# Gate and up projections as Strassen block products, and the down projection as its own stage

## The chip, the core and the metric

The kernel runs on one core of one Trainium2 chip. Its time is the device time of one execution in microseconds (us); three runs of the kernel before the change gave 3655.61 us as their median (3653.2 to 3656.53). The engines named here are TensorE (PE, matmuls; PEld is its loading of weights), VectorE (DVE), ScalarE (ACT), GpSimd (POOL) and SyncE (SP, which issues the loads; ACT issues the stores).

## The reference, cut to what matters

Two blocks run one after the other over 2048 tokens of width 1024. The change lies in the first block, from its output projection to its end:

```
mixed = concat(rmsnorm(ys), rmsnorm(yp))              # 512 + 512 features
h = h + mixed @ w_out                                 # 1024 x 1024
n2 = rmsnorm(h, norm2_g)
ff = silu(n2 @ w_gate) * (n2 @ w_up)                  # 1024 -> 2816 each
h = h + ff @ w_down                                   # 2816 -> 1024
out = rmsnorm(h, final_norm_g)                        # end of the first block
h2 = layer_norm(out, ln_in_g, ln_in_b)                # start of the second
proj = h2 @ w_in_2                                    # attention and linear attention follow
```

## The kernel before

All matrices lie with features on the 128 partitions and tokens along the free axis. A "block" is 512 tokens (`b` = 0 to 3), a "half" is two blocks (`i` = 0, 1), and a feature tile is 128 features (`KT` = 8 tiles of 1024, `NFF` = 22 tiles `j` of 2816). Every product is done to nearly full fp32 precision with three matmuls: each operand is split into a rounded high part and the rest, and `mm3` (L157) issues high by high, high by low, low by high for each k-tile, 128 x 128 weights against 512 tokens.

Weights come through `get_w` (L143) in the order of the generator `weights` (L112): a 512 KB load on SP into `wr` (two buffers), the high part on ACT (`wh`), the low part on POOL, or on DVE where the generator says so (`wl`). The list of instructions on each engine is put in order ahead of time by a scheduler which plays the program against its own timing of each engine; at run time every engine takes its list strictly in that order, and a wait in one instruction holds all behind it.

From 395 to 645 us runs the output projection of the mixer, `mix_out` (L855), one block at a time in the order 2, 3, 0, 1. `mix_in` (L815) loads the eight input tiles of the next block and splits them without the norm's factor; the two halves of the features go to two PSUM tiles, and each is multiplied by its own 1/rms row on the way out. Blocks 0 and 1 keep their result in the SBUF accumulators `hacc`, blocks 2 and 3 go to DRAM (`h1_d`).

From 645 to 2155 us runs the feed-forward part, `ffn_half` (L910) for half 0 and half 1. For each `j` and each block `i`, 24 matmuls make the gate (`pg`), 24 the up product (`pu`), both over eight k-tiles. DVE, ACT and POOL turn them into the hidden tile and split it (`hh`, `hl`). Every second `j`, `down` multiplies the last two hidden tiles by `w_down`: 32 PSUM tiles `dn` of six matmuls, half of them per block, each added on DVE to `hacc` by

```
self.stt(d, pt, 0.5, d, ALU.mult, ALU.add)
```

The hidden tiles never leave SBUF, and the 22 `w_down` tiles are loaded once per half. At the end of a half, `block_norm` (L971) does both norms in place on `hacc` and stores `h2_d`; its pieces are spread over the work that follows by `step`. `ffn_in` (L892) makes the split input of a half: 32 tiles.

From 2155 us on, `proj_half(0, 0)` (L1075) starts the second block.

## Time and profile before

| what | before |
|---|---|
| median of 3 runs | 3655.61 us |
| the profiled execution | 3662.77 us |
| its span, first to last instruction | 3660.8 us |
| PE busy | 3415.1 us (93%) |
| DVE busy | 2038.2 us (56%) |
| ACT busy | 1407.4 us (38%) |
| POOL busy | 1456.0 us (40%) |
| granted TensorE clock, mean | 0.972 |

Busy time of an engine is the union of its records. A matmul's record (some 390 ns for 512 columns) overlaps that of the next, since they are pipelined, so the pace of PE is read from a count over a stretch in which PE never waits, not from the length of a record. A DVE record includes the time in which the instruction was started but held up.

### The profile page before, as it was taken

How to read it: one execution, taken by the hardware profiler on the slowest of the kernel's cores; microseconds unless marked ns; L12 is line 12 of the kernel's file. 1: busy time of each engine (PE TensorE's matmuls, PEld its weight loads, DVE VectorE, ACT ScalarE, POOL GpSimd, SP SyncE). 2: the span in 40 equal slices, each digit the busy share in tenths (PEclk: the TensorE clock that was granted, in tenths of full speed). 3: DMA queues.
4: the chain of work that ended last, by engine and by line, in shares of the span. 5: the costliest groups of instructions: out<-in, count | busy, mean ns of one | idle time of the engine just before them, and what ended most of it. 6: DMA issues, size and time to landing. Idle time of an engine off the chain costs nothing.

```text
span 3660.8 us, 45396 instructions
## 1 busy us (share of the span) xinstructions
PE 3415.1 (93%) x16648; PEld 2838.1 (78%) x16648; DVE 2038.2 (56%) x3431; ACT 1407.4 (38%) x2494; POOL 1456.0 (40%) x1092
## 2 busy tenths in 40 slices
PE   6898798999999998899999989999999999989897
PEld 6687666888888886688888878798888987767676
DVE  7677799433333348533333366234665446787774
ACT  5344544211111125311111154234655445666653
POOL 1255455533343346334333343322322225353544
PEclk9999999999999999999999999999999999989898
DMA  8644554111111122311111135565665666555351
GB/s 246 135 125 117 153 180 130 59 51 48 41 58 46 41 94 91 132 41 58 47 47 51 41 104 190 159 175 171 175 174 148 170 174 174 162 145 157 111 170 51
DMA packets 275490, 424.90 MB, mean 116 GB/s; under 512 B 73506, under 2 KB 159026, under 8 KB 275268
## 3 DMA queue, kind: packets, MB, share of 16 engines
q1 hardware_dynamic: 194880, 334.79, 31.4%
q10 hardware_dynamic: 80388, 87.22, 7.4%
q8 instruction: 131, 2.15, 0.3%
q14 instruction: 91, 0.75, 0.1%
HBM read 324.63 MB, written 87.20 MB: 112 GB/s over the span
## 4 chain that ended last, share of the span: by engine, by line
PE 63%; DVE 15%; DMA 10%; issue 5%; ACT 5%; POOL 1%; SPq 1%; ACTq 0%; DVEq 0%; POOLq 0%
PE pg L161 5%; PE pg L162 5%; PE pg L163 5%; PE pt L163 4%; PE pt L161 4%; PE pt L162 4%; PE pu L161 4%; PE pu L163 4%; PE pu L162 4%; PE dn L161 4%; PE dn L162 4%; PE dn L163 4%; PE pv L1257 2%; PE s L1215 1%; PE pv L1091 1%
## 5 line engine op out<-in xcount | busy, mean ns | idle before, releaser
L44 POOL TENSOR_TENSOR wl<-wr,wh 128x1024 fp32r<-128x1024 f32 (+1 forms) x223 | 548.5, 2466 | 635.9 <-ACT wh L54 590.9
L54 ACT ACTIVATE wh<-wr 128x1024 fp32r<-128x1024 f32 (+2 forms) x297 | 308.0, 1045 | 684.6 <-PE dn L162 197.3
L51 DVE SCALAR_TENSOR_TENSOR hacc<-dn,hacc 128x512 f32<-128x512 f32 x352 | 242.4, 691 | 381.2 <-PE dn L163 379.8
L161 PE MATMUL pg<-xh,wh 128*128 128x512 f32 (+1 forms) x1000 | 390.9, 391 | 15.3 <-ACT t L54 13.6
L162 PE MATMUL pg<-xl,wh 128*128 128x512 f32 (+1 forms) x1000 | 389.2, 389 | 11.3 <-DVE xl L44 6.5
L163 PE MATMUL pg<-xh,wl 128*128 128x512 f32 (+1 forms) x1000 | 388.6, 389 | 1.5 <-POOL wl L44 1.5
L161 PE MATMUL pt<-xh,wh 128*128 128x512 f32 x896 | 358.8, 401 | 7.3 <-DVE t L51 4.3
L163 PE MATMUL pt<-xh,wl 128*128 128x512 f32 x896 | 357.4, 400 | 1.9 <-POOL wl L44 1.4
L162 PE MATMUL pt<-xl,wh 128*128 128x512 f32 x896 | 357.1, 399 | 0.0
L161 PE MATMUL dn<-hh,wh 128*128 128x512 f32 x704 | 278.9, 396 | 20.6 <-DVE hacc L51 13.5
L161 PE MATMUL pu<-xh,wh 128*128 128x512 f32 x704 | 278.6, 396 | 0.0
L162 PE MATMUL pu<-xl,wh 128*128 128x512 f32 x704 | 278.5, 396 | 0.0
L163 PE MATMUL dn<-hh,wl 128*128 128x512 f32 x704 | 275.3, 392 | 3.1 <-POOL wl L44 3.1
L163 PE MATMUL pu<-xh,wl 128*128 128x512 f32 x704 | 278.1, 395 | 0.0
L162 PE MATMUL dn<-hl,wh 128*128 128x512 f32 x704 | 276.1, 392 | 0.0
L48 POOL TENSOR_SCALAR P<-P,rsm 128x640 f32<-128x640 f32 (+4 forms) x128 | 103.3, 807 | 349.7 <-DVE rsm L1225 286.6
L161 PEld LDWEIGHTS pg<-xh,wh 128*128 128x128 f32 x1000 | 190.8, 191 | 59.0 <-ACT t L54 17.2
L162 PEld LDWEIGHTS pg<-xl,wh 128*128 128x128 f32 x1000 | 190.8, 191 | 50.2 <-DVE xl L44 6.9
L163 PEld LDWEIGHTS pg<-xh,wl 128*128 128x128 f32 x1000 | 190.5, 191 | 40.5 <-POOL wl L44 1.9
L44 POOL TENSOR_TENSOR raw<-raw,rb 128x512 f32<-128x512 f32 x88 | 115.2, 1309 | 252.9 <-DVE raw L51 252.9
L44 POOL TENSOR_TENSOR hl<-raw,hh 128x512 fp32r<-128x512 f32 x88 | 114.1, 1297 | 252.8 <-ACT hh L54 252.8
L44 DVE TENSOR_TENSOR t<-pg,rb 128x512 f32<-128x512 f32 x88 | 60.6, 689 | 267.0 <-PE pg L163 266.9
(427 smaller groups left out, 8067.3 us busy)
## 6 DMA issues: line engine op xcount, KB each, us to landing
wr<-in_w_out SPq DMA_DIRECT2D x64, 512.0 KB, 4.3
wr<-in_w_in SPq DMA_DIRECT2D x44, 512.0 KB, 4.0
wr<-in_w_gate SPq DMA_DIRECT2D x44, 512.0 KB, 3.5
wr<-in_w_up SPq DMA_DIRECT2D x44, 512.0 KB, 3.5
wr<-in_w_down SPq DMA_DIRECT2D x44, 512.0 KB, 3.5
raw<-h_d SPq DMA_DIRECT2D x80, 256.0 KB, 4.1
wr<-in_w_ple_gate SPq DMA_DIRECT2D x32, 512.0 KB, 4.0
K<-kh_d SPq DMA_DIRECT2D x48, 256.0 KB, 6.1
```

Source lines behind the costliest of these rows:

```text
L44: return (eng or self.dve).tensor_tensor(out=o, in0=x, in1=y, op=op)
L48: (eng or self.dve).tensor_scalar(out=o, in0=x, scalar1=s1, scalar2=s2, op0=op0, **kw)
L51: return self.dve.scalar_tensor_tensor(out=o, in0=x, scalar=s, in1=y, op0=op0, op1=op1)
L54: return self.act.activation(out=o, in_=x, func=func, **kw)
L161: self.pe.matmul(ps, lhsT=hi[k], rhs=xh[k], start=(first and k == 0), stop=False)
L162: self.pe.matmul(ps, lhsT=hi[k], rhs=xl[k], start=False, stop=False)
L163: self.pe.matmul(ps, lhsT=lo[k], rhs=xh[k], start=False, stop=(last and k == n - 1))
L1091: self.pe.matmul(pt, lhsT=xh, rhs=wlo[:, k % 4], start=False, stop=False)
L1215: self.pe.matmul(sp[:, j, 0:n], lhsT=QQ[:, q0:q0 + 128], rhs=kk[:, k0 + o:k0 + o + n], start=st, stop=not st)
L1257: self.pe.matmul(pv, lhsT=VH[:, kb + x - kt0], rhs=self.PT[m][ch][:, sl], start=(n == 0 and m == 0), stop=(n == len(idxs) - 1 and m == 1))
```

## The change

Gate and up together are one product of a 2 x 2 block matrix (rows: gate, up; columns: the lower and upper 512 input features) with a 2 x 2 block matrix (rows: the same halves of the features; columns: the two token blocks of a half). Strassen's scheme, in Winograd's form, gets the four results from seven block products instead of eight, with additions on the operands before and on the results after. `gu_in` makes the seven token-side operands of a half (56 split tiles instead of 32, each normed ahead of the split), `gu_w` the seven weight-side operands of a tile `j`, one tile ahead, and `gu_half` runs the products: 12 matmuls each, named `pa`, `pb`, `pc` by PSUM bank. `pa` holds the running sum of products 1, 6, 7, 4, and is read between them.

The hidden tiles go to DRAM (`hh_d`, `hl_d`, four stores of 256 KB per `j`). `down` runs after all 22 `j` of a half, one block at a time: it loads the hidden tiles of one `j` back and multiplies them by all eight tiles of `w_down`, which add up in eight PSUM banks over all 22 `j`; only then does DVE add the residual, which comes from DRAM. `w_down` is loaded once per block, four times in all. The result goes to DRAM (`h3_d`), and the final norm (`norm`) reads it from there three times per block, in small steps (`bg_step`) that are placed between the products of the next stage. `gu_in` of half 1 is placed in `down(0)` in the same way, `norm(0)` and `norm(1)` in `gu_half(1)`, `norm(2)` and `norm(3)` in `proj_half(0, 0)`. `mix_out` takes blocks 0 and 1 together, then 2, then 3; the norm's factor is applied to its input tiles, so that one PSUM tile collects all eight k-tiles.

```
+        for j in range(NFF):                       # gu_half
+            w = self.gw
+            nw = self.gu_w(j + 1) if j + 1 < NFF else iter(())
+            pa, pb = bank("pa"), bank("pb")
+            product(pa, 1, True, False)
+            s1 = self.tmp("t", 2)
+            self.fn(s1, pa, AF.Copy)
+            product(pb, 2, True, True)
+            self.tt(s1, pb, s1, ALU.add)
+            h0 = gated(s1)
+            next(nw, None)
+            product(pa, 6, False, False)
+            s2 = self.tmp("t", 2)
+            self.fn(s2, pa, AF.Copy)
+            pc = bank("pc")
+            product(pc, 5, True, False)
+            p5 = self.tmp("raw", 4)
+            self.fn(p5, pc, AF.Copy)
+            next(nw, None)
+            product(pa, 7, False, False)
+            self.tt(p5, pa, p5, ALU.add)
+            product(pc, 3, False, True)
+            self.tt(s2, pc, s2, ALU.add)
+            h1 = gated(s2)
+            next(nw, None)
+            self.tt(h1, h1, p5, ALU.mult)
+            put(1, h1)
+            self.bg_step()
+            product(pa, 4, False, True)
+            self.tt(h0, pa, h0, ALU.mult)
+            put(0, h0)
...
+        put(1, 2, *self.split_in(rg, self.wp, [128, KT, 128], 2, "", None))      # gu_w
+        self.tt(ru[:, lo4], rg[:, lo4], ru[:, lo4], ALU.subtract, eng=self.pool)
...
+        self.tt(s2, ru[:, hi4], ru[:, lo4], ALU.subtract)
...
+        self.halves((th, tl), s2)
+        self.tt(rg[:, lo4], rg[:, lo4], s2, ALU.add)
+        self.tt(rg[:, hi4], rg[:, hi4], s2, ALU.subtract)
...
+        self.halves((sh, sl), rg)
+        put(7, 4, *self.split_in(ru, self.wp, [128, KT, 128], 2, "", None))
...
+            b11, b12, b21, b22 = four                                            # gu_in, for k in range(4)
+            t1 = self.tmp("t", 2)
+            self.tt(t1, b12, b11, ALU.subtract)
+            self.halves(x[1], b11)
+            self.halves(x[2], b21)
+            self.tt(b11, b22, t1, ALU.subtract)
+            self.halves(x[6], b11, self.pool)
+            self.halves(x[5], t1)
+            self.tt(b12, b22, b12, ALU.subtract)
+            self.halves(x[7], b12)
+            self.halves(x[3], b22, self.pool)
+            self.tt(b21, b21, b11, ALU.subtract)
+            self.halves(x[4], b21)
...
+            for j in range(NFF):                                                 # down, for each block
+                hh = self.fp.tile([128, 512], F32R, tag="hh", name="hh", bufs=3)
+                hl = self.fp.tile([128, 512], F32R, tag="hl", name="hl", bufs=3)
+                self.load(hh.bitcast(F32), self.hh_d[b, j])
+                self.load(hl.bitcast(F32), self.hl_d[b, j])
+                hi, lo = self.get_w()
+                for m in range(KT):
...
+                    self.mm3(pss[m], [hi[:, m]], [lo[:, m]], [hh], [hl], first=j == 0, last=j == NFF - 1)
+                if i or j > 1:
+                    self.bg_step()
...
+            for m in range(KT):
+                h = self.tmp("raw", 4)
+                self.load(h, self.h1_d[m * 128:(m + 1) * 128, c])
+                self.stt(h, pss[m], 0.5, h, ALU.mult, ALU.add)
+                self.store(self.h3_d[m * 128:(m + 1) * 128, c], h)
```

What stands on DVE's list in the feed-forward part, before: from one reading of a gate tile to the next but one, with `t<-pg,rb` the reading of a gate, `raw<-raw,t` the gating, `raw<-raw,pu` the product with the up tile, `hacc<-dn,hacc` the adding of a down tile.

```order
L44 TENSOR_TENSOR t<-pg,rb 128x512
L51 SCALAR_TENSOR_TENSOR raw<-raw,t 128x512
L44 TENSOR_TENSOR raw<-raw,pu 128x512
L51 SCALAR_TENSOR_TENSOR hacc<-dn,hacc 128x512 x9
L44 TENSOR_TENSOR t<-pg,rb 128x512
L51 SCALAR_TENSOR_TENSOR raw<-raw,t 128x512
```

Now, in the middle of `gu_half(0)`, one whole tile `j`: `wtl`, `wr`, `sq`, `wsl` are the weight-side operands (`gu_w`).

```order
L44 TENSOR_TENSOR t<-pb,t 128x512
L51 SCALAR_TENSOR_TENSOR raw<-raw,t 128x512
L44 TENSOR_TENSOR wtl<-sq,wth 128x512
L44 TENSOR_TENSOR wr<-wr,sq 128x512 x2
L44 TENSOR_TENSOR sq<-wru 128x512
L44 TENSOR_TENSOR raw<-pa,raw 128x512
L44 TENSOR_TENSOR t<-pc,t 128x512
L44 TENSOR_TENSOR wsl<-wr,wsh 128x1024
L51 SCALAR_TENSOR_TENSOR raw<-raw,t 128x512
L44 TENSOR_TENSOR raw<-raw 128x512
L44 TENSOR_TENSOR raw<-pa,raw 128x512
```

The adding to `hacc` is gone from these lists; four instructions of a tile read PSUM (`pa`, `pb`, `pc`), and eight work from SBUF to SBUF. The same list early in `gu_half(1)`, from the reading of `pb` to the end of the weight-side operands of one tile, with `nh`, `mt`, `sl` of the final norm between them:

```order
L44 TENSOR_TENSOR t<-pb,t 128x512
L51 SCALAR_TENSOR_TENSOR raw<-raw,t 128x512
L44 TENSOR_TENSOR wtl<-sq,wth 128x512
L48 TENSOR_SCALAR mt<-st 128x512
L44 TENSOR_TENSOR wr<-wr,sq 128x512 x2
L44 TENSOR_TENSOR sl<-s,sq 128x512
L51 SCALAR_TENSOR_TENSOR nh<-nh,v_final_norm_g,mt 128x512 x2
L44 TENSOR_TENSOR raw<-pa,raw 128x512
L44 TENSOR_TENSOR t<-pc,t 128x512
L44 TENSOR_TENSOR sq<-wru 128x512
L51 SCALAR_TENSOR_TENSOR nh<-nh,v_final_norm_g,mt 128x512
L44 TENSOR_TENSOR wsl<-wr,wsh 128x1024
```

The norm's instructions stand ahead of those that read PSUM, and are taken first. POOL's list in the feed-forward part before, with `raw<-raw,rb` and `hl` of the hidden tile and `wl` of the weights:

```order
L44 TENSOR_TENSOR raw<-raw,rb 128x512
L44 TENSOR_TENSOR wl<-wr,wh 128x1024
L44 TENSOR_TENSOR hl<-raw,hh 128x512
L44 TENSOR_TENSOR raw<-raw,rb 128x512
L44 TENSOR_TENSOR hl<-raw,hh 128x512
```

And now, across the end of `gu_half(0)` into `down(0)`, where `xl` are operands of half 1 (`gu_in`):

```order
L44 TENSOR_TENSOR wl<-wr,wh 128x1024 x2
L44 TENSOR_TENSOR hl<-raw,hh 128x512 x2
L44 TENSOR_TENSOR wl<-wr,wh 128x1024
L44 TENSOR_TENSOR xl<-raw,xh 128x512 x2
L44 TENSOR_TENSOR wl<-wr,wh 128x1024 x2
```

Two operands of half 1 stand ahead of each of the next pairs of `w_down` tiles, four pairs in all. Last, SP's list as the mixer's output projection begins, before, with `yp_d` and `ys_d` the mixer's two results:

```order
L57 DMA wr<-in_w_out 128x1024 x2
L57 DMA raw<-yp_d 128x512 x4
L57 DMA wr<-in_w_out 128x1024 x2
L57 DMA raw<-ys_d 128x8x64 x4
L57 DMA raw<-in_x 128x512
```

and now:

```order
L57 DMA wr<-in_w_out 128x1024 x4
L57 DMA yr<-yp_d 128x512 x6
L57 DMA wru<-in_w_up 128x1024 x2
L57 DMA yr<-yp_d 128x512 x2
L57 DMA yr<-ys_d 128x8x64 x8
```

All four first tiles of `w_out` stand ahead of `yp_d` now; the third and fourth wait until the first two have been split, since `wr` has two buffers.

## Rows read from the trace of the kernel before

**Rows 1.** Busy time by stretch; columns: start:end, length, engines (x instructions), clock, DMA.

```profile
395.00:645.00 250.00, 206.21 (x811) 157.87 (x810) 223.40 (x235) 123.41 (x173) 136.56 (x84) 0.92 0.52 159
645.00:1340.00 695.00, 695.00 (x3018) 566.70 (x3017) 246.72 (x299) 122.89 (x155) 265.76 (x151) 1.00 0.15 49
1340.00:1430.00 90.00, 83.35 (x354) 65.20 (x352) 74.58 (x89) 47.88 (x72) 54.89 (x33) 1.00 0.39 123
1430.00:1530.00 100.00, 81.66 (x320) 62.79 (x321) 68.53 (x86) 45.44 (x60) 49.62 (x29) 0.91 0.39 133
1530.00:2100.00 570.00, 570.00 (x2476) 464.86 (x2475) 194.62 (x239) 94.29 (x120) 211.54 (x121) 1.00 0.15 49
2100.00:2155.00 55.00, 45.48 (x190) 34.77 (x189) 39.63 (x48) 30.77 (x51) 31.91 (x20) 0.99 0.37 115
2155.00:2310.00 155.00, 148.63 (x802) 128.83 (x803) 88.31 (x123) 57.30 (x108) 56.96 (x41) 0.96 0.45 152
1475.00:1500.00 25.00, 19.58 (x85) 15.56 (x83) 22.70 (x33) 16.74 (x22) 3.79 (x2) 0.97 0.68 232
```

**Rows 2.** The page's chain that ended last, shares by engine.

```profile
PE 63%; DVE 15%; DMA 10%; issue 5%; ACT 5%; POOL 1%; SPq 1%; ACTq 0%; DVEq 0%; POOLq 0%
```

**Rows 3.** Page, groups of instructions; count, busy us, mean ns, idle before and releaser.

```profile
L161 PE MATMUL dn<-hh,wh 128*128 128x512 f32 x704 | 278.9, 396 | 20.6 <-DVE hacc L51 13.5
L161 PE MATMUL pu<-xh,wh 128*128 128x512 f32 x704 | 278.6, 396 | 0.0
```

**Rows 4.** Groups of DVE, POOL, ACT, 645 to 1340 us, shapes apart; columns as rows 3.

```profile
L51 DVE SCALAR_TENSOR_TENSOR hacc<-dn,hacc 128x512 f32<-128x512 f32 x158 | 109.3, 692 | 192.9 <-PE dn L163 192.9
L51 DVE SCALAR_TENSOR_TENSOR raw<-raw,t 128x512 f32<-128x512 f32 x43 | 65.3, 1519 | 31.9 <-ACT raw L54 31.9
...
L44 POOL TENSOR_TENSOR wl<-wr,wh 128x1024 fp32r<-128x1024 f32 x63 | 152.2, 2425 | 172.4 <-ACT wh L54 161.1 <-PE dn L163 11.3
L44 POOL TENSOR_TENSOR raw<-raw,rb 128x512 f32<-128x512 f32 x43 | 56.1, 1304 | 115.1 <-DVE raw L51 115.1
L44 POOL TENSOR_TENSOR hl<-raw,hh 128x512 fp32r<-128x512 f32 x42 | 54.1, 1288 | 132.6 <-ACT hh L54 132.6
...
L54 ACT ACTIVATE wh<-wr 128x1024 fp32r<-128x1024 f32 x63 | 65.8, 1058 | 264.2 <-PE dn L162 92.8 <-DMA wr<-in_w_up 56.0 <-PE pg L162 45.5
```

**Rows 5.** DVE in order of time: start us, us, instruction; one `j`, then the mixer.

```profile
1018.33 2.47 DVE L51 SCALAR_TENSOR_TENSOR raw<-raw,t 128x512 f32<-128x512 f32 x1 [0.76 <-ACT raw L54]
...
1031.44 0.69 DVE L51 SCALAR_TENSOR_TENSOR raw<-raw,t 128x512 f32<-128x512 f32 x1 [0.70 <-ACT raw L54]
...
554.20 1.21 DVE L44 TENSOR_TENSOR wl<-wr,wh 128x1024 fp32r<-128x1024 f32 x1
...
557.36 1.82 DVE L44 TENSOR_TENSOR hacc<-hacc,raw 128x512 f32<-128x512 f32 x1
```

**Rows 6.** POOL in order of time at the same places.

```profile
1017.85 2.40 POOL L44 TENSOR_TENSOR wl<-wr,wh 128x1024 fp32r<-128x1024 f32 x1 [1.14 <-ACT wh L54]
...
554.85 1.70 POOL L44 TENSOR_TENSOR s<-s,sq 128x512 f32<-128x512 f32 x1 [0.62 <-ACT sq L54]
...
557.33 1.30 POOL L44 TENSOR_TENSOR s<-s,sq 128x512 f32<-128x512 f32 x1 [0.78 <-ACT sq L54]
```

**Rows 7.** The loads as the mixer's output projection begins, SP in order of time.

```profile
394.79 0.87 SPq L57 DMA_DIRECT2D wr<-in_w_out  x2
395.71 1.88 SPq L57 DMA_DIRECT2D raw<-yp_d  x4
```

**Rows 8.** Page, DMA issues: count, KB each, median us from issue to landing.

```profile
wr<-in_w_down SPq DMA_DIRECT2D x44, 512.0 KB, 3.5
raw<-h_d SPq DMA_DIRECT2D x80, 256.0 KB, 4.1
```

**Rows 9.** What PE waited for, 1400 to 2160 us: total us, times, longest.

```profile
PE dn L161 <- DVE hacc L51: 11.7, 5, 6.7
PE dn L161 <- ACT wh L54: 6.8, 2, 6.6
PE pv L1090 <- DVE hacc L51: 4.6, 1, 4.6
```

More of the change, by code (lines that the diff above doesn't have):

```diff
@@ L966, in load_acc, with bg_step @@
[L966 to L979 removed]
+    def bg_step(self, n=1):
+        while n and self.bg:
+            if next(self.bg[0], None) is None:
+                self.bg.pop(0)
+            else:
+                n -= 1
@@ new lines, in gu_prime, with gu_half, product, bank @@
+    def gu_prime(self):
+        self.gu_raws = [self.gu_raw(0)]
+        for _ in self.gu_w(0):
+            pass
+    def gu_half(self, half):
+        def product(ps, p, first, last):
+            hi, lo = w[p]
+            x = self.xg[p]
+            ks = range(4)
+            for k in ks:
+                for n, (l_, r_) in enumerate(((hi, 0), (hi, 1), (lo, 0))):
+                    self.pe.matmul(ps, lhsT=l_[:, k], rhs=x[k][r_], start=(first and k == n == 0),
+                                   stop=(k == 3 and n == 2), skip_group_check=True)
+        def bank(name):
+            return self.ps.tile([128, 512], F32, tag="ps", name=name, bufs=8)
+        def gated(g):
+            th = self.tmp("raw", 4)
+            self.fn(th, g, AF.Tanh, scale=0.5)
+            self.stt(th, th, 1.0, g, ALU.add, ALU.mult)
+            return th
+        def put(i, h):
+            hh = self.fp.tile([128, 512], F32R, tag="hh", name="hh", bufs=3)
+            hl = self.fp.tile([128, 512], F32R, tag="hl", name="hl", bufs=3)
+            self.split(hh, hl, h)
+            self.store(self.hh_d[2 * half + i, j], hh.bitcast(F32))
+            self.store(self.hl_d[2 * half + i, j], hl.bitcast(F32))
+        for j in range(NFF):
[25 more added lines that the diff above has]
+            put(1, h1)
+            self.bg_step()
+            product(pa, 4, False, True)
+            self.tt(h0, pa, h0, ALU.mult)
+            put(0, h0)
+            next(nw, None)
+            self.bg_step()
+            if j == NFF - 1:
+                self.w_all = self.weights(f"down{half}")
+                self.w_next.append(self.get_w(0))
@@ L1094, in tokens @@
                     done(cb, t0 + t * 128, pt)
+                    if half == part == 0:
+                        self.bg_step()
         def put_v(cb, t, pt):
```

417 lines of the change are left out of this document (233 added, 184 removed).

## Prediction

> **What bounds the kernel now.** I read the table of stretches first [rows 1]. From 645 to 1340 us and from 1530 to 2100 us PE is busy all the time at full clock while DVE, ACT and POOL are all under 40%: the feed-forward part is bound by the number of matmuls. Around the turn of the halves and at the end PE lacks 6.7 + 18.3 + 9.5 = 34 us of 245. The mixer's output projection, 395 to 645 us, is another matter: PE lacks 44 of 250 us and its clock averages 0.92 of 2.4 GHz, while DVE is busy 223 us and POOL 137 us, together more than the stretch is long. The chain [rows 2] gives PE 63% and DVE 15%, which fits a kernel with one long matmul stage and DVE in the short ones.
>
> The pace of PE: 695.00 us / 3018 matmuls = 0.2303 us each [rows 1]; the 390 ns of a record [rows 3] overlap.
>
> DVE and POOL shut each other out. A gating instruction from SBUF to SBUF takes 0.69 us alone, and 2.47 us when POOL has begun a 2.40 us split 0.5 us before it [rows 5, 6]: it ends 0.55 us after POOL does. It holds the other way too: a sum on POOL takes 1.30 us alone and 1.70 us beside the 1.21 us split on DVE [rows 5, 6]. Instructions that read PSUM are not held: the 158 adds to `hacc` mean 692 ns with POOL at 38%, the gating 1519 ns [rows 4]. So for two-input work in SBUF the two engines have one budget. The mixer's stretch confirms it: the lists hold 124 narrow DVE instructions for it (512 columns, 0.69 us) and 32 wide ones (1024 columns, 1.21), and with 84 POOL sums (1.29) they add up to 233 us of 250.
>
> **The matmuls.** Per tile `j` of a half, 7 products x 12 = 84 matmuls replace 96; 12 x 44 tiles = 528 fewer, x 0.2303 = **-121.6 us**. The down matmuls stay 2112, the mixer's 768. A tile `j` now lasts 84 x 0.2303 = 19.35 us, one `j` of `down` 24 x 0.2303 = 5.53 us.
>
> **The old waits go.** 645 to 2155 us is 1510 us; 6336 matmuls x 0.2303 = 1459. The other **-51 us** (waits, slower clock, column sums at the turns; for what PE waited see rows 9) belong to `hacc`, whose tiles had to be ready before the next adds and norms. The 352 adds of 0.69 us on DVE go too, beside PE in any case, worth nothing by themselves. What takes the place of both is costed below.
>
> **The mixer's output projection: +15 us.** By the same budget: 113 narrow and 12 wide on DVE, 52 sums and 12 splits (2.43) on POOL = 78 + 15 + 67 + 29 = 189 us, plus `gu_in(0)` with 52 on DVE and 8 on POOL = 46, plus the first weights of `gu_w`, 12: 247 us against 233, 14 more. Added to it, the `yp_d` loads, which began at 395.7 us [rows 7], now stand behind two more weight loads that wait for a split: some 5 us; taken off, the last operands, which PE needs a few products later: 4 us. Bounds: -20 (the budget was not quite full before, and PE has 44 us of waits to lose) to +35.
>
> **`gu_half(0)`: +3 us of waits.** Per tile, POOL has two wide splits, one narrow subtraction and two splits of hidden tiles: 2 x 2.43 + 1.30 + 2 x 1.29 = 8.7 us [rows 4]; DVE has seven narrow and one wide from SBUF, 7 x 0.69 + 1.21 = 6.0. That is 14.8 us of budget in 19.35 us; the four PSUM readers, 2.8 us, run beside POOL. It fits, at 77%. The hand-offs are tight: `pa` must be copied or read before the next product adds to it, within one product of 2.76 us, behind whatever stands ahead on DVE. One wide POOL split in the way costs 2.4 us. PE's list has pieces of the next tile's products 1 and 2 put in between, which roughly doubles the slack. Bounds 0 to 40 us (2 us per tile).
>
> **`gu_half(1)`: +52 us of waits.** Here `norm(0)` and `norm(1)` are laid over 14 of 22 tiles. They bring 88 narrow DVE instructions from SBUF and 28 sums on POOL: 88 x 0.69 + 28 x 1.29 = 97 us. In the lists, ten of the 14 tiles carry nearly all, 8.6 on DVE and 2.8 on POOL each: 14.8 + 5.9 + 3.6 = 24.3 us of budget for 19.35 us of matmuls, so these tiles are bound by DVE and POOL: 10 x 5.0 = 50, and a little for the column sums in PE's list. Bounds: 0 (the lists let the norms fall behind) to 110 (DVE also waits for PSUM in order, 3 us more per tile, and more at the sums).
>
> One rule of the Trainium skill speaks against this stage. With rows first: where PE was busy 82% its mean clock was 0.92 and 0.91, a mixture of 1.2 and 2.4 GHz, and where it was busy 93% it was 1.00 [rows 1]. The Trainium skill ("TensorE: Matmul & The Clock Gate", section "A second HAM failure mode: psum-queue depth-cycling") says that a kernel which cycles through PSUM banks and idles briefly between groups of matmuls can have its clock swing between half and full. By it the ten loaded tiles, busy 19.35 / 24.3 = 80%, would run at 0.92, and the sum would be up to 17 us higher if PE and not DVE set their length; by the budget alone it costs nothing, since the clock only fills PE's waits.
>
> **`down`.** PE has no partner that must follow each tile any more. Loads are 2 x 256 KB of hidden tiles and 512 KB of weights per 5.53 us, 190 GB/s; the trace shows 232 GB/s at 68% of the DMA engines [rows 1], and loads land in 3.5 and 4.1 us [rows 8] with two tiles of lead, so I cost the way through DRAM at nothing; each microsecond short per `j` would cost 88. The weights' split, 1.06 + 2.43 us [rows 4] after a buffer comes free, fits in 5.53. But `gu_in(1)` stands in `down(0)`: per k-tile 13 narrow on DVE and two on POOL, with two weight splits between, 9.0 + 2.6 + 4.9 = 16.5 us against two `j` of 11.1, and POOL's list makes the `w_down` splits wait behind it. Three of the four k-tiles bite: **+15 us** (0 to 35). `down(1)` has 16 light loads: +3. The eight evictions at the end of each block (0.69 us each from PSUM, residual loads with four buffers): 4 x 3 us, and 3 us where `gu_in(0)` meets the first products: **+15** (5 to 30).
>
> **After 2155 us: +3 us.** `norm(2)`, `norm(3)` run beside `proj_half(0, 0)`, where PE was busy 149 of 155 us: 88 narrow and 28 sums are 97 us of budget, with twelve wide splits 29 more, still under 155.
>
> **The sum.** -121.6 - 51 + 15 + 3 + 52 + 15 + 3 + 15 + 3 = -66.6 us. Against the profiled execution's 3662.8 us: 3596. The runs' median lies 7.2 us below that execution, so **3589 us**.
>
> **Rivals.**
> A. The norms and `gu_in` fall behind without holding PE, as every off-path engine did in the 695 us without a wait [rows 1]. For: nothing of the norms is needed by a product. Against: they share DVE's list with readers of `pa` that PE waits for. The 52, the 15 and half of the rest go: about 3515 us.
> B. Slower than before: the hand-offs over `pa` and `pc`. Each tile has four points where PE may not go on before ACT or DVE has read the bank, and on DVE these reads stand behind SBUF work that POOL can hold for 2.4 us at a time. The gain of 121.6 + 51 is paid back from 67 us more of waits on, that is 1.5 us per tile over 44 tiles. At one held instruction, 2.4 us, on each tile: +106 us, 3695. For: DVE [rows 5] was held for most of POOL's split when they met. Against: such meetings cost PE nothing before, and the new PE list has more lead.
> C. `down` becomes bound by its loads or by the chain of split and buffer, for example 6.2 us per `j`: 88 x 0.67 = +59, 3648. For: twice the loads, all on SP's list behind one another. Against: rows 1 and 8.
> D. The clock: if short waits at every tile bring the gate and up stages to the 0.92 of the stretches at 82% [rows 1], they take 44 x 19.35 x 0.087 = 74 us more, 3663. For: the 0.91 and 0.92 themselves. Against: single waits there were up to 6.7 us long [rows 9], and the waits forecast here are shorter. That is the rule of the page named above, carried through the whole stage.
>
> **How the numbers follow.** Forecast 0.50, A 0.18, B 0.17, C 0.09, D 0.06. The likeliest one's own range is 3545 to 3640, from the bounds above, since they will not all fall on one side. For 8 in 10, I take half of A and reach past C to the near part of B: 3535 to 3670. A measurement of this kernel can tell about 0.2%, 7 us, from no change. Faster: the forecast nearly whole, A, about half of C and a quarter of D: 0.74. Within 0.2%: 0.06, from C and D. Slower: B and the rest: 0.20.
>
> **What would show it.** Right: 84 matmuls per tile at 0.230 us; tiles of 19.4 to 20 us in `gu_half(0)`; about ten tiles of 24 to 25 us in the first 14 of `gu_half(1)` and 19.4 after; DVE gating and `nh` instructions there well over 1 us; three waits of `dn` matmuls on POOL's `wl` early in `down(0)`. Wrong: equal tiles in both halves (A), tiles over 21 us in `gu_half(0)` with PE waiting for DVE or ACT on `pa` (B), 5.8 us or more per `j` in the bare part of `down` (C), or a clock under 0.97 in `gu_half` without long waits (D).

## The result, and the profile after

The changed kernel is slower: 3719.17 us (median of 4 runs, 3709.14 to 3722.14) against 3656.07, ratio 1.0169 with a 95% interval of 1.0149 to 1.0189. The forecast was 3589 us, and the range ended at 3670.

The ends of the stages are read from the first and last start of a tile's matmuls. Columns: line, engine, operation, count, duration in ns (least, median, most), first and last start in us.

```profile
L163 PE MATMUL mo<-xh,wh x256: 387/394/796, 430.2 to 715.3; 128*128 128x512 f32 x128
...
L1039 PE MATMUL pa<-xh,wh x528: 387/394/796, 728.2 to 1916.7; 128*128 128x512 f32 x176
...
L163 PE MATMUL dn<-hh,wh x704: 388/394/797, 1180.9 to 2177.4; 128*128 128x512 f32 x176
...
L1264 PE MATMUL pv<-wh,xh x512: 274/283/579, 2190.6 to 2995.4; 128*128 128x264 f32 x86, 128*128 128x256 f32 x85
```

In both kernels the mixer's own products end near 400 us, and the stage is counted from 395; the first `pa` is at 728.2, where the feed-forward part of before began at 645.7, and `pv`, the first product of the second block, is at 2190.6 instead of 2155.3. The spans are 3720.4 and 3660.8 us. So the three parts are:

| part | before | after | change | forecast |
|---|---|---|---|---|
| mixer's output projection, from 395 us | 250.7 | 333.2 | +82.5 | +15 |
| feed-forward part | 1509.6 | 1462.4 | -47.2 | -84.6 |
| behind it | 1505.5 | 1529.8 | +24.3 | +3 |
| sum | | | +59.6 | -66.6 |

The stretches of the changed kernel, with the columns of [rows 1]:

```profile
395.00:430.00 35.00, 4.59 (x13) 2.68 (x14) 12.96 (x17) 14.27 (x24) 9.93 (x7) 0.60 0.48 150
430.00:540.00 110.00, 80.97 (x281) 61.35 (x281) 56.03 (x68) 35.49 (x56) 33.88 (x22) 0.82 0.40 110
540.00:728.00 188.00, 126.51 (x509) 99.61 (x509) 112.31 (x121) 61.72 (x90) 73.80 (x43) 0.85 0.46 141
728.00:778.00 50.00, 45.82 (x174) 35.54 (x174) 39.44 (x47) 21.61 (x34) 25.30 (x11) 0.88 0.24 79
778.00:1147.00 369.00, 369.00 (x1595) 299.15 (x1595) 229.56 (x230) 144.77 (x208) 177.74 (x94) 1.00 0.32 110
...
1181.00:1446.00 265.00, 252.88 (x1055) 203.01 (x1056) 62.91 (x64) 61.56 (x72) 121.79 (x53) 0.97 0.64 213
1451.00:1762.00 311.00, 284.56 (x1177) 224.41 (x1176) 252.17 (x261) 146.68 (x215) 172.73 (x95) 0.97 0.47 151
1762.00:1898.00 136.00, 136.00 (x589) 110.38 (x588) 83.64 (x83) 52.54 (x76) 64.58 (x34) 1.00 0.30 105
1918.00:2178.00 260.00, 251.16 (x1056) 201.63 (x1056) 38.69 (x39) 62.23 (x72) 119.76 (x53) 0.97 0.69 226
2191.00:2385.00 194.00, 168.68 (x874) 143.53 (x874) 95.36 (x139) 62.41 (x113) 66.35 (x50) 0.92 0.59 184
```

The new matmul stages look as forecast: in `gu_half(0)` PE never waits for 369 us, in `gu_half(1)` it waits in the part with the norms (285 of 311 us busy) and not behind it. The loss stands in the first three rows. There PE is busy 212 of 333 us, DVE 181, POOL 118 and the DMA engines 44%: nothing is full.

What PE waited for from 395 to 728 us, after (us in total, times, longest):

```profile
PE st L746 <- ACT sq L54: 91.4, 8, 26.2
PE mo L163 <- ACT xh L54: 16.7, 3, 5.8
```

and from 395 to 645.5 us, before:

```profile
PE mo L161 <- DVE t L44: 16.3, 3, 10.4
...
PE st L741 <- ACT sq L54: 0.8, 2, 0.5
```

`st` is the column sum, two small matmuls that add the squares over the partitions. Its first matmul waited 0.8 us before and waits 91.4 us now: 44 us at the sums over the inputs, 47 us at those over the outputs. How that comes about is seen where the stage begins, in order of time:

```profile
407.82 0.63 ACT L54 ACTIVATE s<-yr 128x512 f32<-128x512 f32 x1 [8.54 <-DMA yr<-yp_d]
...
409.05 3.95 POOL L44 TENSOR_TENSOR s<-s,sq 128x512 f32<-128x512 f32 x3 [10.13 <-ACT sq L54]
...
413.71 0.79 PE L746 MATMUL st<-sq,ones_r 128*128 128x512 f32 x1 [14.94 <-ACT sq L54]
...
418.83 2.74 DVE L51 SCALAR_TENSOR_TENSOR yr<-yr,v_pool_norm_g,t 128x512 f32<-128x512 f32 x4
...
421.49 2.49 DVE L44 TENSOR_TENSOR xl<-yr,xh 128x512 fp32r<-128x512 f32 x4
...
429.62 0.80 PE L746 MATMUL st<-sq,ones_r 128*128 128x512 f32 x1 [14.40 <-ACT sq L54]
...
430.22 0.63 PE L163 MATMUL mo<-xh,wh 128*128 128x512 f32 x1
...
439.60 1.22 PE L163 MATMUL mo<-xh,wh 128*128 128x512 f32 x2 [5.07 <-ACT xh L54]
```

A block's operands are now scaled by 1/rms ahead of the split, so the chain load, squares, sums, column sum, 1/rms, scaling, split stands in front of its products. The first half of block 0's operands is ready at 424 us, but PE's list has the column sum of block 1 next, and PE stands until 429.6. The longest wait is at the end of block 2, at the sum over its outputs:

```profile
641.02 1.27 DVE L44 TENSOR_TENSOR t<-mo,raw 128x512 f32<-128x512 f32 x2
...
647.90 0.69 DVE L44 TENSOR_TENSOR t<-mo,raw 128x512 f32<-128x512 f32 x1 [5.60 <-DMA h_d<-t]
...
656.49 0.69 DVE L44 TENSOR_TENSOR t<-mo,raw 128x512 f32<-128x512 f32 x1 [3.12 <-DMA raw<-h_d]
...
665.87 0.80 PE L746 MATMUL st<-sq,ones_r 128*128 128x512 f32 x1 [26.25 <-ACT sq L54]
...
670.73 0.63 PE L164 MATMUL mo<-xl,wh 128*128 128x512 f32 x1
...
671.15 0.63 PE L165 MATMUL mo<-xh,wl 128*128 128x512 f32 x1
...
671.85 0.40 PE L164 MATMUL mo<-xl,wh 128*128 128x512 f32 x1
...
672.09 0.40 PE L165 MATMUL mo<-xh,wl 128*128 128x512 f32 x1
```

PE has run seven output tiles ahead. DVE reads them late: its list has `gu_in`'s work first, each output tile `t` (two buffers) is free again only when its store has landed, and at 656.49 the read had waited for a load. Until the last is read, squared and added, PE stands 26 us at the column sum with the products of block 3 queued behind it.

### The profile page after: what moved, and what is told of

Read it like the earlier page. It is cut to its first block, busy times and chain, and to the rows that moved or that the text cites. A ratio compares the mean times of both kernels' runs of the same rounds, so it can differ in the third digit from the quotient of the medians.

```text
span 3720.4 us, 46121 instructions
## 1 busy us (share of the span) xinstructions
PE 3342.3 (90%) x16120; PEld 2766.1 (74%) x16120; DVE 2127.1 (57%) x3427; ACT 1567.7 (42%) x2740; POOL 1537.5 (41%) x1088
## 5 line engine op out<-in xcount | busy, mean ns | idle before, releaser
L1039 PE MATMUL pa<-xh,wh 128*128 128x512 f32 x528 | 214.1, 405 | 28.8 <-ACT t L54 18.4
L1039 PE MATMUL pa<-xl,wh 128*128 128x512 f32 x528 | 211.7, 401 | 2.2 <-DVE xl L44 2.2
L163 PEld LDWEIGHTS pt<-xh,wh 128*128 128x128 f32 x896 | 170.9, 191 | 53.2 <-DVE hl L51 5.8
L1039 PE MATMUL pa<-xh,wl 128*128 128x512 f32 x528 | 209.2, 402 | 0.9 <-POOL wl L44 0.9
L44 POOL TENSOR_TENSOR s<-s,sq 128x512 f32<-128x512 f32 x94 | 134.6, 1432 | 160.8 <-ACT sq L54 156.2
L165 PEld LDWEIGHTS pt<-xh,wl 128*128 128x128 f32 x896 | 170.3, 190 | 37.8 <-DVE wl L44 1.4
L164 PEld LDWEIGHTS pt<-xl,wh 128*128 128x128 f32 x896 | 170.7, 190 | 35.1 <-issue 0.7
L163 PEld LDWEIGHTS dn<-hh,wh 128*128 128x128 f32 x704 | 136.0, 193 | 65.4 <-DMA hh<-hh_d 15.2
L51 DVE SCALAR_TENSOR_TENSOR raw<-dn,raw 128x512 f32<-128x512 f32 x32 | 20.9, 685 | 274.4 <-PE dn L165 246.9
L1264 PE MATMUL pv<-wh,xh 128*128 128x256 f32 (+1 forms) x512 | 149.1, 293 | 25.5 <-DVE raw L51 12.4
L164 PEld LDWEIGHTS dn<-hl,wh 128*128 128x128 f32 x704 | 135.5, 192 | 33.8 <-DMA hl<-hl_d 2.1
```

What stands on the lines that cost most here:

```text
L44: return (eng or self.dve).tensor_tensor(out=o, in0=x, in1=y, op=op)
L51: return self.dve.scalar_tensor_tensor(out=o, in0=x, scalar=s, in1=y, op0=op0, op1=op1)
L163: self.pe.matmul(ps, lhsT=hi[k], rhs=xh[k], start=(first and k == 0), stop=False)
L164: self.pe.matmul(ps, lhsT=hi[k], rhs=xl[k], start=False, stop=False)
L165: self.pe.matmul(ps, lhsT=lo[k], rhs=xh[k], start=False, stop=(last and k == n - 1))
L1039: self.pe.matmul(ps, lhsT=l_[:, k], rhs=x[k][r_], start=(first and k == n == 0), stop=(k == 3 and n == 2), skip_group_check=True)
```

## The experiments

All ratios are to the kernel before, run beside each of them, with 95% intervals; the changed kernel has 1.0169. Stages in us, from the profiled run: "mixer" from 395 us to the first product of gate and up, the next four from the first to the last start of their matmuls (`pg` and `pu` in e4 and e18), "to attention" from the first `pv` to the first score product.

| run | ratio | mixer | gu_half(0) | down(0) | gu_half(1) | down(1) | to attention |
|---|---|---|---|---|---|---|---|
| the change | 1.0169 | 333.2 | 442.2 | 265.2 | 469.2 | 256.1 | 194.1 |
| e1_ring6 | 1.0114 (1.0095-1.0133) | 317.2 | 444.2 | 266.9 | 469.6 | 253.2 | 191.0 |
| e2_sums | 1.0195 (1.0175-1.0216) | 316.8 | 462.2 | 265.1 | 469.2 | 259.2 | 198.3 |
| e3_nonorm | 0.9980 (0.9970-0.9990) | 326.9 | 440.4 | 264.8 | 429.1 | 254.8 | 157.7 |
| e4_eight | 1.0332 (1.0313-1.0351) | 320.7 | 491.6 | 253.3 | 502.1 | 252.2 | 193.3 |
| e5_factor | 1.0156 (1.0138-1.0174) | 322.2 | 445.6 | 266.4 | 469.4 | 256.5 | 200.0 |
| e6_rings | 1.0139 (1.0121-1.0156) | 319.3 | 438.3 | 264.3 | 468.1 | 257.7 | 203.1 |
| e7_nh6 | 1.0165 (1.0146-1.0184) | 338.0 | 442.2 | 264.5 | 468.0 | 257.5 | 174.7 |
| e8_spread | 1.0160 (1.0145-1.0175) | 335.1 | 442.6 | 263.2 | 459.7 | 257.2 | 192.5 |
| e10_noss | 1.0065 (1.0041-1.0089) | 279.3 | 453.9 | 266.0 | 471.7 | 257.4 | 192.1 |
| e11_nors | 0.9949 (0.9934-0.9964) | 246.9 | 440.9 | 265.9 | 472.5 | 255.2 | 202.7 |
| e12_small | 1.0095 (1.0078-1.0112) | 328.9 | 443.4 | 267.5 | 462.0 | 258.8 | 170.2 |
| e13_oldmix | 1.0058 (1.0037-1.0079) | 299.8 | 436.6 | 267.3 | 471.0 | 254.1 | 199.1 |
| e14_latesum | 1.0064 (1.0043-1.0086) | 283.4 | 443.1 | 268.9 | 470.2 | 257.1 | 203.0 |
| e15_all | 0.9982 (0.9971-0.9993) | 280.9 | 444.3 | 269.3 | 460.3 | 263.0 | 172.6 |
| e16_all2 | 0.9966 (0.9955-0.9978) | 272.0 | 453.0 | 270.3 | 463.0 | 260.3 | 171.9 |
| e17_nochain | 0.9992 (0.9979-1.0004) | 257.2 | 441.2 | 265.3 | 471.8 | 260.0 | 197.2 |
| e18_best8 | 1.0161 (1.0142-1.0181) | 268.0 | 492.3 | 259.7 | 514.7 | 255.9 | 178.5 |
| e19_early | 1.0002 (0.9990-1.0015) | 283.3 | 449.1 | 269.8 | 462.9 | 262.4 | 170.8 |

e7 and e8 do not touch the mixer, and it took 338.0 and 335.1 us in them: some 5 us of a stage differ from run to run. Behind it the spread is wider: eleven of these kernels (the change, e1, e2, e4, e5, e6, e10, e11, e13, e14, e17) have the same code from the first `pv` to the end, and took from 1513 (e1) to 1537 us (e6) for it.

### What the products gained

**e4_eight.**

```
-            pa, pb = bank("pa"), bank("pb")
-            product(pa, 1, True, False)
...
+                for ps, (hi, lo) in ((pg, w[0]), (pu, w[1])):
+                    self.mm3(ps, [hi[:, k] for k in ks], ...)
```

> Strassen's scheme is undone and all else kept: gate and up by eight block products (96 matmuls per tile j), plain operands in gu_in (32 split tiles) and gu_w (two splits), hidden tiles through DRAM, down, mixer and norms as in the changed kernel. 528 more matmuls at 0.2303 us are 121.6 us. Theory (the products gained what was forecast, the rest of the change lost it): 3719 + 121.6 less the waits of gu_half(1) that the lighter DVE and POOL take away, 20 to 44 us, less some 10 us of gu_in: about 3795 (3770 to 3840). Rival (the additions and splits of Strassen's operands cost what its products gain): 3720 to 3750.

The ratio rises by 0.0163, 60 us, which lies in the theory's range and 21 us below its figure. The two stages of gate and up take 993.7 us instead of 911.4, a difference of 82 of the 121.6 us; the mixer and `down(0)`, which hold the plain and lighter `gu_in`, give 12 back each. So the scheme gained about half of its matmuls, and the rest of the change lost some 120 us.

### The norms beside other stages

**e3_nonorm.** `norm` becomes load, scaling on ACT, store.

> The norms between the blocks are left out: each tile of h3_d is loaded, scaled by a constant on ACT and stored to h2_d, so DVE's and POOL's share of norm and its column sums are gone, one pass of loads stays of three. Theory (the prediction's, that the norms over gu_half(1) and proj_half(0,0) are paid in PE's waits): gu_half(1) falls from 469.6 us to about the 442.7 of gu_half(0), the stretch from the first pv product to the first attention product from 194 to about 160 us, and the time to about 3660. Rival (the two halves of gate and up differ for another reason, the hand-offs of pa): gu_half(1) stays above 460 us, and only what stands behind 2190 us is gained, 3690.

As expected, and 15 us beyond it in the time: `gu_half(1)` falls by 40 us to the pace of `gu_half(0)`, the way to the attention by 36 us to about what it took before the change (159.7). The norms cost about 70 us where they stand.

**e7_nh6.**

```
-            t = self.fp.tile([128, 512], F32, tag="nh", name="nh", bufs=2)
+            t = self.norm_tile(b)          # b > 1: nh, nh, wth, wtl, wsh, wsl in turn
```

> One edit: the tiles of norm(2) and norm(3) rotate over six buffers instead of two (four are weight tiles that are idle after gu_half). Theory (beside proj_half(0,0) the norms are bound by the turn of two buffers, 24 pairs of tiles, each a load of 3.6 us, the work and in the last pass a store, and the attention can only start when they are through): the stretch from the first pv product to the first attention product falls from 194 to about 165 us, PE's waits there from 37 to under 25 us, the time to about 3694. Rival (the budget of DVE and POOL, or PE's waits for the column sums): the stretch stays above 186 us, time within 8 us of 3719.

The stretch shrinks by 19 of the theory's 29 us, and the time stays, as the rival has it. The stretches from the first `pv` to the first score product and from there to the end, after and in e7:

```profile
2190.60:2384.70 194.10, 168.75 (x872) 143.63 (x873) 95.36 (x139) 62.41 (x113) 66.35 (x50) 0.92 0.59 184
2384.70:3720.40 1335.70, 1237.36 (x6818) 1055.16 (x6818) 815.80 (x1551) 709.04 (x1408) 497.14 (x439) 0.96 0.53 155
```

```profile
2194.40:2369.10 174.70, 155.20 (x823) 133.76 (x824) 105.13 (x137) 58.51 (x109) 67.89 (x49) 0.94 0.60 193
2369.10:3715.70 1346.60, 1249.96 (x6867) 1065.40 (x6867) 812.12 (x1553) 710.89 (x1412) 493.39 (x440) 0.96 0.54 155
```

The earlier attention leaves 49 matmuls for the stage behind it, 49 x 0.2303 = 11 us, which lasts 10.9 us longer. What is left, 8.5 us less from `pv` to the end, is hardly above what the intervals can tell.

**e8_spread.**

```
-                        self.bg = [self.norm(0), self.norm(1)] if half else []
+                        if half:
...
+                            self.bg = [self.take(n0, 6), self.take(n1, 10)]
...
+                            self.bg, more = [self.gu_in(1)], self.take(n0, 4)      # down(0)
+                            self.bg, more = [self.take(n0, 4), self.take(n1, 4), self.proj_in_steps()], self.take(n2, 4)
```

> The norms are spread: the first pass of norm(0) runs in the second block of down(0), the last passes of norm(0) and norm(1) in the first block of down(1) ahead of the loads for the projection, the first pass of norm(2) in its second block; gu_half(1) keeps the second pass of norm(0) and two passes of norm(1), one step per tile instead of two. DVE was busy 39 of 260 us in down(1). Theory (the norms cost PE time where DVE and POOL are already loaded, not where they are idle): gu_half(1) falls from 469 to about 450 us, down(0) and down(1) stay within 4 us of 265 and 256, the stretch behind 2190 us falls by 8 to 15 us; time about 3690. Rival (each norm costs its waits wherever it stands, through PSUM banks and column sums): time within 8 us of 3719.

Half a hit: `gu_half(1)` gains 9.5 us and the down stages lose nothing, but the way to the attention stays, bound by its two buffers. **e12_small** joins e1, e7 and e8.

> Three earlier edits together: six buffers for mix_out's outputs (ratio to before 1.0114 by itself), six for the tiles of norm(2) and norm(3) (1.0165), the norms spread over the down stages (1.0160), against 1.0169 of the changed kernel. If the three add up: ratio 1.0101, about 3690. Theory (with the ring widened, the spread first pass of norm(2) lets the norms end earlier, so the attention starts earlier): 1.006 to 1.009. Rival (what one gives, the stages behind take back): 1.011 to 1.014.

1.0095, where the sum of the three is 1.0101: the edits add up, within the intervals. With the buffers and the earlier start together the attention begins 170 us after `pv`.

### The mixer: buffers, places, work or chain

**e1_ring6.**

```
-                xr, h = self.tmp("raw", 4), self.tmp("t", 2)
+                xr, h = self.tmp("raw", 4), self.out_tile()   # t, t, wth, wtl, wsh, wsl in turn
```

> One edit: the output tiles h of mix_out rotate over six buffers instead of the two of t (four of them are weight tiles of gu_w that are idle there). In the changed kernel PE waits 91 us in eight waits for column sums between 395 and 730 us, and DVE waits 20.9 us for stores from t to land. Theory 1 (the sums are late because the evictions wait for the two buffers): the eight waits fall from 91 to about 50 us and the time to about 3680. Theory 2 (the sums are late because of their place in PE's list, right behind the last product of their block, with a chain of squares and POOL sums behind the last eviction): the list of PE is the same, so the waits stay above 75 us and the time within 12 us of 3719. Theory 3 (the budget of DVE and POOL of the prediction is what holds the stage): no change within 5 us.

Between the theories: the sums' waits fall by only 9 us, to 83, the stage by 16. The buffers are one of the links. The ratio gives 20 us, the two profiled executions differ by 32; 13 of these lie behind the first score product, where nothing was edited, and within the spread named above. **e6_rings** gave the residual loads two buffers of their own on top of it.

> On top of the six output buffers of the first run (3694): the residual loads of mix_out get two buffers of their own (idle weight tiles) and no longer share the four raw buffers with mix_in and gu_in, in which the load queue waited 22.5 us at 653 us. Theory (what is left of the stage's loss is buffers that are held): the stage, 317 us there, shrinks by 10 to 25 us more, time 3670 to 3685. Rival (the chain of evictions, sums, 1/rms, DRAM and gu_in itself): within 6 us of 3694.

The rival holds for the stage, which stays. The time is 14 us above e1's, more than the rival's 6: behind `pv` e6 and e1 are the two ends of the spread.

**e2_sums.**

```
+            if m == 2:
+                self.late_sums()            # column sums of the blocks before
-            if (m or not start) and m < steps:
+            if (m or not start) and (m < steps if steps == 8 else m == 4):
```

> One edit: the column sums at the end of each mix_out are emitted three products later (after product m = 2 of the next mix_out, for block 3 in the first tile of gu_half(0)); gu_in's steps in mix_out move from m = 0 to m = 4, since they need these sums. Theory 2 (place in PE's list): the waits for column sums between 395 and 730 us fall from 91 to under 40 us, and the time by 40 to 60 us, to about 3670. Theory 1 (evictions held by the two buffers of t): PE meets the same late evictions as waits for PSUM banks instead, and the time falls by 20 us at most. Theory 3 (budget): no change within 5 us.

My second theory falls: the waits for sums fall to 72 us and not under 40, the mixer gains 16 us, and `gu_half(0)` loses 20. `gu_in(0)` needs these sums, its steps were moved with them, and it is late now: PE waits 15.5 us there for its `xh` and `xl`. In this stage the sums at the outputs are not free to move.

**e5_factor.**

```
+                self.tt(t, p1, self.rs[b, 1], ALU.mult)
+                self.tt(h, p0, self.rs[b, 0], ALU.mult)
+                self.tt(xr, xr, t, ALU.add, eng=self.pool)
+                self.tt(h, h, xr, ALU.add)
```

> One part of the change undone: in the mixer's output projection the norm's factor is applied on the way out again, as before the change (unnormed operands split at once, two PSUM tiles per block and product, each times its own 1/rms row, 32 more POOL sums and 64 more DVE instructions); block order, DRAM route of h1 and gu_in stay as in the changed kernel. Theory (the stage became long because the chain load, squares, sum, column sum, 1/rms, scaling, split now stands ahead of the first products of blocks 0 and 1, where PE waits 53 us between 395 and 490 us): the stage from 395 us to the first product of gu_half(0) shrinks from 333 by 25 to 40 us and the time to about 3685. Rival (the end of the stage, where gu_in(0) needs r2 and h1, sets its length): less than 10 us of gain, or a loss from the added work of DVE and POOL.

The first product starts 10 us earlier (420.3), and no more is gained. The waits for `st` are 94.2 us, since the column sums still stand early in PE's list. Where the factor is applied is not the point.

**e10_noss** and **e11_nors** each cut one half of the statistics out.

> Left out: the squares and sums of mix_out's outputs, their four column sums and the rows r2 in DRAM; gu_in takes a constant in place of 1/rms. Theory (end chain: late evictions, sum, column sum, 1/rms, DRAM, gu_in hold PE behind 540 us): the waits of 9.8, 26.2 and 11.4 us of the changed kernel go and their slow restart with them; the stage from 395 us shrinks from 333 by 40 to 55 us, time about 3675. Rival (the evictions themselves are late, whatever reads them): the stage shrinks by less than 20 us, PE waits for PSUM banks or for xh of gu_in instead.

> Left out: the squares, sums and column sums of mix_in's inputs; the inputs are scaled by a constant in place of 1/rms, with the same scaling and splitting instructions. Theory (start chain: the first products of blocks 0 and 1 wait for loads, squares, sums, column sum, 1/rms before the scaling): the waits of 14.9, 14.4, 5.1, 5.8, 5.8 us before 480 us shrink to one of some 10 us for loads and splits, and 2.4, 2.4 and 9.8 us later go; the stage shrinks by 40 to 60 us, time about 3670. Rival (DVE's and POOL's budget): only 32 squares on ACT and 24 sums of 1.29 us on POOL go, 31 us of 333, half of which PE sees: 10 to 15 us.

Both theories hold, the second beyond its size: without the outputs' statistics the stage is 54 us shorter, and without the inputs' it takes 246.9 us, 86 less, all that the change had added. Work or chain? **e17_nochain** puts the work back and leaves the chain cut:

```
-        ps = self.total(s)                  # and the 1/rms row made of it
+        self.dve.memset(r, 0.5)             # squares and sums of s stay
```

> As the run without the norm of the inputs (ratio 0.9949, stage 246.9 us), but the 32 squares on ACT and 24 sums on POOL of mix_in stay; left out are only what follows them: the eight column sums on PE, the splits of the sums and the 1/rms rows, with a constant in their place. Theory (the chain through PE's list is what costs): the stage stays at 250 to 262 us, ratio 0.995 to 0.999. Rival (the budget of DVE and POOL: the squares and sums are the cost): the stage goes back by most of the 86 us, to above 290 us, ratio above 1.007.

The stretch in e11 and in e17:

```profile
395.00:642.00 247.00, 196.50 (x795) 154.43 (x795) 143.81 (x174) 85.27 (x123) 84.46 (x49) 0.90 0.59 182
```

```profile
395.00:652.00 257.00, 194.12 (x785) 151.23 (x786) 157.45 (x170) 101.31 (x153) 120.19 (x72) 0.89 0.55 171
```

POOL has its 36 us back and ACT 16; DVE is busy 14 us longer with no more work on its list. The stage is 10 us longer: of the 86 us, 76 go with the chain and 10 with the squares and sums. The chain takes DVE's work for the sums' splits and the 1/rms rows with it, 24 us of DVE's busy time (181 to 157); if all of that held PE, some 50 us would still be waiting. What is left in e17 are the sums over the outputs:

```profile
PE st L746 <- ACT sq L54: 36.7, 3, 12.7
```

So the cause is that PE stands at column sums, and not a full engine. The 76 us here and the 54 of e10 add up to more than the 82.5 that were lost; how far the two chains hide each other is not shown, as no run cuts both.

**e13_oldmix** takes the mixer of before, with the old places of its sums: squares from product m = 1 on, column sums at m = 6.

```
+            if nxt is not None and m == 1:
+                self.xin = self.mix_in(nxt)
+            if nxt is not None and m == 6:
+                self.mix_stat(self.xin[1], 0)
```

> The mixer's output projection as before the change (one block at a time, inputs of the next block loaded and split during this one, two PSUM tiles per product from three tags, a PSUM bank of its own for column sums, factors on the way out), only in the block order 0 to 3, with every output going to h1_d, and with gu_in(0) placed in blocks 2 and 3; everything after it as in the changed kernel. Theory (the rebuilt stage itself lost the time: order of the chains and PSUM banks shared with the column sums): from 395 us to the first product of gu_half(0) 270 to 290 us instead of 333, 250 of before and 20 to 40 for gu_in(0); time 3660 to 3675. Rival (what loses the time is gu_in(0) and the way of h1 through DRAM): above 315 us, time above 3700.

299.8 us, between the two; of the 33.4 us of waits for `st` that are left, 26.6 fall on the last block's own column sum, at the turn. **e14_latesum** moves that sum into the first tile of `gu_half(0)`.

> The mixer as before the change (ratio 1.0058, stage 299.8 us), with the column sum of the last block moved into the first tile of gu_half(0). Theory (that sum alone held PE for 21.6 + 5.0 us at the turn): stage about 272 us, gu_half(0) within 6 us of 436.6, ratio 0.998 to 1.000. Rival (gu_in(0), with half its steps behind the last product, is late by itself, as when the sums were moved in the changed kernel): gu_half(0) takes back 15 us or more, ratio 1.003 to 1.006.

Neither quite: the stage is 16 us shorter, but PE now waits 15.1 us at the first `pa` for a PSUM bank that DVE has not read, and `gu_half(0)` takes 6.5 us back: no gain in time. The evictions are late, whoever asks for them.

### Does it add up?

**e15_all** is e14 with the edits of e7 and e8 and one more, and **e16_all2** is e15 with more buffers and a quarter of the mixer's weight splits on POOL; in e15 the first hidden tile of `down` goes to `wsh`, `wsl`:

```
+                if j or i: hh, hl = ...     # as they were
+                else: hh, hl = ...          # wsh, wsl
```

> The last one with three more edits: six buffers for the tiles of norm(2) and norm(3), the norms spread over the down stages, and the first hidden tile of each down stage loaded into two idle weight tiles (PE waited 10.1 and 4.2 us for it). If the accounts add up: 0.999 less 15 us for norms (sum of the three small edits was 27 us with the output ring's 22) and less 8 us for the turns, ratio 0.992 to 0.995, faster than the kernel before. Rival (given back behind): 0.997 or more.

> The last one with every second output tile of mix_out in two idle wide tiles instead of the two of t, and one of four weight splits of the mixer on POOL instead of DVE (PE waited 1 to 3.5 us at a time for splits on DVE and for banks that DVE had not read). Theory: 5 to 10 us less than e15. Rival (DVE's list is not what holds the stage by then): within 5 us of it.

e15 gains 30 us on e14 and ends where the rival had it: the attention starts 30 us sooner after `pv`, and the stage behind it is 18 us longer; the two turns shrink from 10.8 and 4.7 to 3.7 and 0.3 us. e16 gains 5 us more, the low end of its theory, and the intervals of the two overlap. It is the fastest kernel that computes all, 3646.56 us, 0.9966 (0.9955 to 0.9978) of the kernel before. Its stages, columns as [rows 1]:

```profile
395.00:667.00 272.00, 213.15 (x811) 162.25 (x810) 241.77 (x253) 123.61 (x176) 164.13 (x95) 0.90 0.55 171
667.00:1120.00 453.00, 434.73 (x1849) 350.25 (x1850) 292.50 (x293) 177.91 (x255) 217.69 (x116) 0.97 0.33 113
...
1394.00:1858.00 464.00, 441.91 (x1861) 352.65 (x1862) 313.37 (x354) 205.27 (x298) 232.72 (x127) 0.98 0.41 135
```

DVE and POOL are busy far longer in this mixer (242 and 164 us against 181 and 118) and it is 61 us shorter. **e19_early** moved `gu_in(0)` two products forward, and **e18_best8** undid Strassen's scheme in e16.

> The best version so far with the four steps of gu_in(0) moved two products earlier (after products 2 and 5 of block 2, 1 and 4 of block 3, instead of 3 and 7 of each). Theory (gu_half(0) starts late because its last operands are): gu_half(0) falls from 453 to about 443 us, ratio 0.993 to 0.995. Rival (the steps hold the evictions of mix_out on DVE's list instead): the stage ahead grows by what is gained, ratio 0.996 to 0.998.

> The best version so far (mixer as before the change with its last column sum moved, norms spread, more buffers; ratio 0.9966) with Strassen's scheme undone: eight products of 12 matmuls per tile. In the changed kernel undoing it cost 55 us net. Theory (the gain of the products stands by itself): 50 to 70 us slower than that version, ratio 1.010 to 1.016. Rival (the lighter operands repair the start of gu_half(0) and the second down stage): 25 us or less, ratio below 1.004.

e19: the rival, and worse, 1.0002: the mixer grows by 11 us and `gu_half(0)` gives back 4. e18: 0.0195 of the time, 71 us, a little above the theory. Whether the scheme gains more here than the 60 us of e4, the intervals do not tell.

## Why the prediction was wrong, point by point

**The step that failed: "the mixer's output projection, +15 us".** It took the stage for bound by the budget of DVE and POOL, because 233 us of narrow and wide instructions nearly filled 250, and it added 14 us for a list of 247. It measured +82.5. e17 is the test: with all squares and sums of the inputs in place and only their column sums and 1/rms rows cut, the stage is 257 us. The busy times of [rows 1], 223 + 137 us in a stretch of 250, were no sign of a full budget: a DVE record includes the time in which it is held, and in e16 the same two are busy 242 + 164 us in 272. The prediction named the move of the `yp_d` loads (5 us) and took off 4 us for "the last operands", and did not ask how much time each column sum has. Before, five products, 5 x 24 x 0.2303 = 27.6 us, stood between the squares of a block's inputs and their column sum; now 48 matmuls, 11 us, and for blocks 0 and 1 none, by the order in the new `mix_in` and `mix_out`. The sums over the outputs come on top, 47 of the 91 us; the longest of them hangs on evictions that stand behind `gu_in(0)`'s work and wait for the two buffers of `t`. Bounds of -20 to +35 came from the same budget, and so missed as well.

The Trainium skill ("Perfetto Trace Analysis", section "Roofline") says that a kernel with low matmul and low memory utilisation is bound by latency, by stalls and dependencies. The trace of the changed stage agrees: PE is busy 64%, the DMA engines 44%, and 76 us go with the chain.

**The matmuls, -121.6, and the old waits, -51: right.** 16120 matmuls are 528 fewer. These two products of `pb` are 19 tiles apart:

```profile
777.59 0.39 PE L1039 MATMUL pb<-xh,wl 128*128 128x512 f32 x1
...
1147.12 0.39 PE L1039 MATMUL pb<-xh,wl 128*128 128x512 f32 x1
```

369.53 / 19 = 19.45 us, forecast 19.35 and "19.4 to 20". That rules rival B out (over 21).

**`gu_half(0)`, +3: +17.** 442.2 us from first to last start against 22 x 19.35 = 425.7. Ten of the 17 are lost in the first 50 us, where the last operands of `gu_in(0)` come and the clock is 0.88 (174 matmuls, 40 us at the full pace, from 728 to 778); in the 369 us behind, the hand-offs over `pa` cost nothing.

**`gu_half(1)`, +52: +44, and e3 gives 40.** Fourteen tiles from 1450.87 to 1762.49 us take 22.3 us each, the others 19.4. A is ruled out. The budget served here, where DVE was busy 81% and POOL 56%. The sign named for it told nothing: the gating took 1107 ns there and 1086 in `gu_half(0)`. PE waited mostly for ACT's copy of `pa` (18.1 us in seven waits), not for column sums.

**Rival D** fell: with PE busy 285 of 311 us the clock was 0.97, and 1.00 behind. In these 311 us 37 of the 1177 matmuls start 0.43 us after the one before and not 0.23, 36 of them in four pieces behind waits of 2.6 to 4.8 us: some 7 of the 40 us are the clock. [rows 1] has a stretch against D that the prediction passed over: from 2100 to 2155 us PE was busy 83%, and the clock was 0.99. Of the rule of the Trainium skill that stood beside D ("TensorE: Matmul & The Clock Gate", section "A second HAM failure mode: psum-queue depth-cycling") this stage shows those 7 us and no more.

**`down(0)`, +15, `down(1)`, +3, evictions and turns, +15: 22, 13 and 30.** Without waits a block's `j` takes 5.55 us (450 matmuls in 104.0 us, from 1946 to 2050), forecast 5.53, so C is ruled out; e4 puts the lighter `gu_in(1)` at 12 us. But the waits on POOL's `wl` came to 0.3 us; PE waited for `hh` and ACT's `wh`. The turns were sized too small: 10.1 and 4.2 us of waits for the first hidden tile from DRAM, 12.4 for the last evictions. The 10.1 are in part SP's list: the load began at 1174.4 us, 4 us after the last product, behind loads that waited for other stores to land, and took 6.5 us. "I cost the way through DRAM at nothing" holds within a stage and not at its ends.

**After 2155 us, +3: +24.** The budget again: 97 + 29 us of work under 155. The norms' three passes go through two buffers, and what SP's loads waited for from 2190 to 2385 us shows it, after and in e7 (us in total, times, longest):

```profile
SPq L57 <- DMA h_d<-nh: 66.8, 15, 15.0
```

```profile
SPq L57 <- DMA h_d<-nh: 35.7, 9, 21.2
```

The attention starts when they are through: 194 us after `pv` instead of 160. Ten of these 34 us come back behind it. The 24 us stand against a spread of 1513 to 1537 us among kernels with the same code there, so their size is known to some 12 us only.

So 68 of the 126 us between forecast and result are the mixer, 37 the starts and turns of the feed-forward stages, 21 what lies behind. No rival had this: B forecast a slower kernel, but by hand-offs over `pa`, which cost nothing where they were watched for 369 us. What remains open: why the mixer of before takes 300 us and not 250 with `gu_in(0)` beside it, what the stage would be with both chains cut, and what makes the spread behind `pv`.

## What to carry to other kernels

A budget of busy time bounds a stage only where an engine is near full in it; where all are half idle, write out the chain from the first load to the first product and count what stands in the in-order list between a value's start and the instruction that waits for it. A small matmul that waits for a sum stops every product behind it, so it needs as many products ahead of it as the sum takes, or a producer that does not hang on late evictions. A saving in one stage is only had if the stages at its ends can start as early, so cost the first load and the last eviction of every new stage by themselves.

## What the runs showed of the hardware

A long wait costs more than its length. After the 26.25 us at 665.87 the matmuls started 0.43 us apart for twelve of them, and 0.23 us apart from 671.85 on (rows of the result): about 2.5 us more. From 395 to 728 us 801 matmuls made PE busy for 212 us, 0.265 each; the granted clock was 0.60 to 0.85, a mixture of 1.2 and 2.4 GHz. Some 83 matmuls of the stage start at the slow pace, and 48 in the stage before the change, which makes 17 and 10 us: 7 of the 82.5 us lost are the clock, nearly all the rest waits. The forecast of the mixer had no such term.
